# At both gate-and-up starts the third product is moved up behind the fifth, with its operand made straight from PSUM

## The chip, the cores and the metric

The kernel runs on one core of one Trainium2 chip. TensorE (PE in the profile) multiplies into PSUM; VectorE (DVE) and ScalarE (ACT) do elementwise work; SyncE (SP) issues most of the transfers. The metric is device time in microseconds (us) for one execution; lower is better. Before the change the median of three runs is 2316.03 us (2315.48 to 2316.67).

## The reference

One decoder layer is computed in float32, for 1024 positions of width 1024: a gated feed-forward block (width 2816), a mixer, a second feed-forward block, a final normalisation. The change touches only the start of the two feed-forward blocks:

```python
def swiglu(h, w_gate, w_up, w_down):
    a = jnp.einsum("bld,df->blf", h, w_gate)
    b = jnp.einsum("bld,df->blf", h, w_up)
    return jnp.einsum("blf,fd->bld", jax.nn.silu(a) * b, w_down)
...
    x = x + 0.5 * swiglu(rms_norm(x, ffn1_norm[i]), ffn1_w_gate[i], ffn1_w_up[i], ffn1_w_down[i])
...
    x = x + 0.5 * swiglu(rms_norm(x, ffn2_norm[i]), ffn2_w_gate[i], ffn2_w_up[i], ffn2_w_down[i])
```

## The kernel before, in words

**Seven products in place of eight.** Every gate or up multiplication is cut into 2 x 2 blocks and done by Strassen and Winograd's scheme. The normalised input gives blocks r11 and r21 (first half of the positions, first and second half of the features, made in `b_first`) and r12 and r22 (second half of the positions, in `b_second`), and sums of them are the right operands of products 1 to 7; `b_op(H, m)` holds operand m as a rounded float32r part (`bh`) and the rest (`bl`). The weights give left operands the same way (`ah`, `al`), made by `a_ops`. One product is four steps of three matmuls 128x512 (bh by ah, bl by ah, bh by al), twelve in all, and at a start each product is done twice, for the gate and for the up weights: 24 matmuls.

**Banks and running sums.** A product adds into a PSUM bank. Products 1 and 2 share a bank `x` (`ps_pj`). Product 5 goes to bank `z` (gate in `ps_pj`, up in `ps_oo`), is copied out by ScalarE as `r` (L417), and product 3 is later added into the same bank z; so product 3 may write there only after that copy has read it. Before the change products 7 and 4 add into bank `w` (`ps_mx`) and product 6 has a bank `y` of its own (`ps_sc`); VectorE then forms u = y + t1, w = w + u, r = w + r from PSUM.

**The start of a feed-forward block.** `first_products` does products 1 and 2 from the first half of the positions. `b_second` handles the second half: for each of four k it transposes two 128x512 blocks on TensorE (L228, into the two `ps_sc` banks), forms the operands of products 5 and 7 from the first transpose (L300, L304, L306), stores r22 (L302) from the second, and then makes the operands of products 6, 3 and 4 from r11, r22 and r21. `between(0)` and `between(1)` stand for `a_start` with n = 2 and 3, which make the weight operands of the next products, and the loads of the next weight blocks (`a_load`, L325). `gate_up_all` then holds the first gate and up pair by itself (its first loops), before the loop over the 20 further half-blocks. This start occurs twice: near 37 us for the first block (called ffn1 here) and near 1675 us for the second (ffn2).

**What sets the order.** Every engine runs its own list of instructions in order. The kernel is recorded in program order, and a scheduler of the framework then chooses the order in which the instructions stand on each engine, within the bounds that `tc.issue_after` sets. So the two calls of the same functions need not come out in the same order at ffn1 and at ffn2. Pools limit buffers: two `ps_sc`, two `ps_mx`, three `ps_pj`, one `ps_oo`; two buffers each for `ah` and `al`, so the weights of product 4 wait until the matmuls of an earlier group of weights have ended.

Of the kernel before, what the change touches and what calls it, by code (L numbers as in the profile page):

```python
# [11 lines left out]
F32 = mybir.dt.float32  # L12
# [9 lines left out]
P = 128  # L22
# [22 lines left out]
def kernel(  # L45
# [17 lines left out]
    def psum(tag):  # L63
        return ps.tile([P, 512], F32, name="ps_" + tag, tag=tag, bufs=PS_BUFS[tag])
# [159 lines left out]
    def transposed(xns, k):  # L224

        pt = psum("sc")
        for i in range(4):
            T.transpose(pt[:, i * P:(i + 1) * P], xns[i][:, k * P:(k + 1) * P], ident)  # L228
        return pt
# [60 lines left out]
    def b_second(pool, H_ops, x1, wcol, H, r11, r21, r22, between):  # L290

        def put(m, k, src):
            return split2(b_op(H, m)[0][:, k], b_op(H, m)[1][:, k], src)

        first_products(pool, H, H_ops)
        for k in range(4):
            p12 = transposed(x1, k)
            w = wcol[:, k:k + 1]
            t1 = pool.tile([P, 512], F32, name="bs", tag="q")
            V.scalar_tensor_tensor(out=t1, in0=p12, scalar=w, in1=r11[:, k], op0=ALU.mult, op1=ALU.subtract)  # L300
            put(5, k, t1)
            A.mul(out=r22[:, k], in_=transposed(x1, k + 4), mul=wcol[:, k + 4:k + 5])  # L302
            t3 = pool.tile([P, 512], F32, name="bs", tag="q")
            V.scalar_tensor_tensor(out=t3, in0=p12, scalar=w, in1=r22[:, k], op0=ALU.mult, op1=ALU.subtract)  # L304
            hi, lo = put(7, k, t3)
            V.tensor_tensor(out=r11[:, k], in0=r11[:, k], in1=t3, op=ALU.subtract)  # L306
        with tc.issue_after(hi.ins), tc.issue_after(lo.ins):
            between(0)
            for k in range(4):
                put(6, k, r11[:, k])  # L310
            t4 = []
            for k in range(4):
                hi, lo = put(3, k, r22[:, k])
        with tc.issue_after(lo.ins):
            for k in range(4):
                t4.append(pool.tile([P, 512], F32, name="bs", tag="q"))
                V.tensor_tensor(out=t4[k], in0=r21[:, k], in1=r11[:, k], op=ALU.subtract)
        between(1)
        for k in range(4):
            last = put(4, k, t4[k])  # L320
        return last

    def a_load(w, p):
# [4 lines left out]
    def a_ops(pool, *prods):  # L328

        hi = wp.tile([P, 4, 4, P], F32R, name="ah", tag="whi")  # L330
        lo = wp.tile([P, 4, 4, P], F32R, name="al", tag="wlo")
        near = {}
        for i, (raw, m, ops) in enumerate(prods):
            a11, a12 = raw[:, 0:4, 0:P], raw[:, 4:8, 0:P]
            a21, a22 = raw[:, 0:4, P:2 * P], raw[:, 4:8, P:2 * P]

            def summed(x, y, op):
                t = pool.tile([P, 4, P], F32, name="as", tag="q")
                V.tensor_tensor(out=t, in0=x, in1=y, op=op)
                return t  # L340

            if m == 5:
                v = near[id(ops)] = summed(a21, a22, ALU.add)
            elif m == 6:
                if id(ops) in near:
                    v = summed(near[id(ops)], a11, ALU.subtract)
                else:
                    v = summed(a21, a11, ALU.subtract)
                    V.tensor_tensor(out=v, in0=v, in1=a22, op=ALU.add)
                ops["s2"] = v  # L350
            elif m == 7:
                v = summed(a21, a11, ALU.subtract)
            elif m == 3:
                v = summed(a12, ops["s2"], ALU.subtract)
            else:
                v = {1: a11, 2: a12, 4: a22}[m]
            last = split2(hi[:, i], lo[:, i], v)
            ops[m] = hi[:, i], lo[:, i]
        return last


# [6 lines left out]
    def prod(H, bank, ops, m, first=False):  # L368
        (wh, wl), (bh, bl) = ops[m], H[m]
        for k in range(4):  # L370
            a, z = first and k == 0, k == 3
            T.matmul(bank, lhsT=wh[:, k], rhs=bh[:, k], start=a, stop=False, skip_group_check=True)  # L372
            T.matmul(bank, lhsT=wh[:, k], rhs=bl[:, k], start=False, stop=False, skip_group_check=True)  # L373
            T.matmul(bank, lhsT=wl[:, k], rhs=bh[:, k], start=False, stop=z, skip_group_check=True)  # L374
        return bank

    def first_products(pool, H, ops):

        for st in ops:
            st["x"] = prod(H, psum("pj"), st, 1, True)  # L380
            st["t1"] = pool.tile([P, 512], F32, name="m1f")
            A.copy(out=st["t1"], in_=st["x"])
        for st in ops:
            prod(H, st["x"], st, 2)

    def gate_up_all(pool, H, w_gate, w_up, scr, raws, ops, work, tail):
# [6 lines left out]
        def wtile(gate, name):  # L393
            return work.tile([P, 512], F32, name=name, tag="sg" if gate else "mu", bufs=8 if gate else 3)
# [21 lines left out]
            st["r"] = wtile(gate, "r")  # L416
            A.copy(out=st["r"], in_=st["z"])  # L417
        for st in ops:
            st["w"] = prod(H, psum("mx"), st, 7, True)
        for st in ops:  # L420
            st["y"] = prod(H, psum("sc"), st, 6, True)
        for gate, st in zip((True, False), ops):
            st["u"] = wtile(gate, "u2")
            plus(st["u"], st["y"], st["t1"])
            plus(st["w"], st["w"], st["u"])
            plus(st["r"], st["w"], st["r"])
            prod(H, st["z"], st, 3)
        ready((2, 1), (2, 5), (2, 6), (2, 2))
        for st in ops:
# [1086 lines left out]
```

## Time and profile before

| what | value |
|---|---|
| median of three runs | 2316.03 us |
| the profiled execution, its own time | 2315.88 us |
| its span (first to last instruction) | 2314.2 us |
| mean TensorE clock granted | 0.997 of full speed |

One execution is profiled. Its span is 1.7 us below its own time. The profile's page gives for each engine the busy time, the share of the span and the number of instructions, then the span in 40 slices, the chain of work that ended last, and the costliest groups of instructions. The trace behind it can be asked for every instruction in order of time: start, duration, engine, line, operation, tiles out and in, shapes, and in square brackets how long the engine had been idle and what released it. A count such as x2 means that equal neighbours were merged. Matmul durations overlap; what a stream of them costs is read from the distance of their starts.

### The profile page before, as it was taken

To read this page: it belongs to the slowest core of one execution; us is meant where nothing else is said; L and a number is where in the kernel's file an instruction comes from. 1 tells how busy PE (TensorE), PEld (TensorE's weight loads), DVE (VectorE), ACT (ScalarE), POOL (GpSimd) and SP (SyncE) were. 2 spreads that over 40 slices of the span, in tenths; PEclk is the share of its full clock that TensorE was granted. 3 is DMA by queue.
4 is the path that set the end of the run, shared out by engine and by line. 5 is a ranking of instruction groups with operands and counts; after the bars stand their busy time and mean duration, and the time that the engine had idled before them with its cause. 6 is when DMAs were issued, how large, how long until landed. Compare 5 with 4: busy or idle time off the path is not lost.

```text
span 2314.2 us, 31020 instructions
## 1 busy us (share of the span) xinstructions
PE 2270.9 (98%) x11718; PEld 1858.6 (80%) x11718; DVE 1623.5 (70%) x3181; ACT 1082.6 (47%) x1872; POOL 54.0 (2%) x125
## 2 busy tenths in 40 slices
PE   6999999999999999999999999999999999999998
PEld 4888888888878888878788787788878888888886
DVE  7765666667775675668878788888596666656787
ACT  7333333343367785863545555432453333334344
POOL 0000000000000000000000000000000000000000
PEclk9999999999999999999999999999999999999999
DMA  3332323574653322232333322335222323349446
GB/s 111 105 118 92 114 96 109 186 282 124 207 180 99 92 92 61 69 102 74 83 101 75 81 81 58 119 100 190 91 87 96 109 96 110 100 140 327 138 154 214
DMA packets 231435, 281.40 MB, mean 122 GB/s; under 512 B 57448, under 2 KB 164044, under 8 KB 230260
## 3 DMA queue, kind: packets, MB, share of 16 engines
q1 hardware_dynamic: 231028, 279.31, 37.8%
q8 instruction: 92, 1.51, 0.3%
q14 instruction: 59, 0.48, 0.1%
q0 software_dynamic: 256, 0.10, 0.0%
HBM read 211.59 MB, written 67.77 MB: 121 GB/s over the span
## 4 chain that ended last, share of the span: by engine, by line
PE 85%; DVE 8%; ACT 3%; DMA 2%; issue 1%; SPq 0%; POOL 0%; DVEq 0%; ACTq 0%
PE ps_pj L123 9%; PE ps_pj L121 9%; PE ps_pj L122 9%; PE ps_mx L372 5%; PE ps_mx L374 5%; PE ps_mx L373 5%; PE ps_pj L372 3%; PE ps_pj L373 3%; PE ps_pj L374 3%; PE ps_sc L373 3%; PE ps_sc L374 3%; PE ps_sc L372 3%; PE ps_pj L583 2%; PE ps_pj L584 2%; PE ps_pj L582 2%; DMA wst<-in_ffn_w_down_dram 1%
## 5 line engine op out<-in xcount | busy, mean ns | idle before, releaser
L121 PE MATMUL ps_pj<-hhi,whi 128*128 128x512 f32 x832 | 334.3, 402 | 0.8 <-ACT gsb L855 0.8
L123 PE MATMUL ps_pj<-hhi,wlo 128*128 128x512 f32 x832 | 334.4, 402 | 0.0
L122 PE MATMUL ps_pj<-hlo,whi 128*128 128x512 f32 x832 | 331.9, 399 | 0.0
L372 PE MATMUL ps_mx<-bh,ah 128*128 128x512 f32 x512 | 199.4, 390 | 0.0
L373 PE MATMUL ps_mx<-bl,ah 128*128 128x512 f32 x512 | 199.2, 389 | 0.0
L374 PE MATMUL ps_mx<-bh,al 128*128 128x512 f32 x512 | 199.2, 389 | 0.0
L123 PEld LDWEIGHTS ps_pj<-hhi,wlo 128*128 128x128 f32 x832 | 156.7, 188 | 29.6 <-issue 1.9
L121 PEld LDWEIGHTS ps_pj<-hhi,whi 128*128 128x128 f32 x832 | 156.8, 188 | 29.2 <-ACT gsb L855 1.3
L122 PEld LDWEIGHTS ps_pj<-hlo,whi 128*128 128x128 f32 x832 | 156.7, 188 | 29.2 <-issue 1.2
L251 ACT CAST ah<-as 128x512 fp32r<-128x512 f32 x176 | 104.4, 616 | 114.1 <-PE ps_mx L373 106.4
L251 ACT CAST hid<-hraw 128x1024 fp32r<-128x1024 f32 (+1 forms) x84 | 82.4, 981 | 155.3 <-PE ps_oo L584 49.1
L251 ACT CAST ah<-wst 128x512 fp32r<-128x512 f32 x132 | 77.4, 618 | 150.6 <-PE ps_sc L373 122.8
L372 PE MATMUL ps_pj<-bh,ah 128*128 128x512 f32 x368 | 145.1, 395 | 2.7 <-ACT r L417 1.1
L373 PE MATMUL ps_pj<-bl,ah 128*128 128x512 f32 x368 | 144.5, 393 | 0.0
L374 PE MATMUL ps_pj<-bh,al 128*128 128x512 f32 x368 | 143.9, 391 | 0.0
L373 PE MATMUL ps_sc<-bl,ah 128*128 128x512 f32 x336 | 132.8, 395 | 5.3 <-DVE bl L252 5.3
L372 PE MATMUL ps_sc<-bh,ah 128*128 128x512 f32 x336 | 132.4, 394 | 2.0 <-ACT ah L251 2.0
L374 PE MATMUL ps_sc<-bh,al 128*128 128x512 f32 x336 | 132.2, 393 | 0.0
L252 DVE TENSOR_TENSOR hid<-hraw,hid 128x1024 fp32r<-128x1024 f32 (+1 forms) x84 | 95.0, 1131 | 47.3 <-ACT hid L251 46.8
L252 DVE TENSOR_TENSOR al<-as,ah 128x512 fp32r<-128x512 f32 x176 | 116.9, 684 | 3.5 <-ACT ah L251 1.0
L372 PEld LDWEIGHTS ps_mx<-bh,ah 128*128 128x128 f32 x512 | 96.1, 188 | 20.5 <-ACT u L469 0.5
L374 PEld LDWEIGHTS ps_mx<-bh,al 128*128 128x128 f32 x512 | 96.1, 188 | 19.9
(445 smaller groups left out, 5176.4 us busy)
## 6 DMA issues: line engine op xcount, KB each, us to landing
hraw<-hid_scr SPq DMA_DIRECT2D x70, 512.0 KB, 3.7
hid_scr<-hs SPq DMA_DIRECT2D x110, 256.0 KB, 6.4
wst<-in_ffn_w_down_dram SPq DMA_DIRECT2D x50, 512.0 KB, 4.8
wst<-in_ffn_w_gate_dram SPq DMA_DIRECT2D x22, 1024.0 KB, 6.6
wst<-in_ffn_w_up_dram SPq DMA_DIRECT2D x22, 1024.0 KB, 5.4
wst<-in_w_in_dram SPq DMA_DIRECT2D x36, 512.0 KB, 4.8
keep<-in_ffn_w_down_dram SPq DMA_DIRECT2D x20, 512.0 KB, 6.5
wst<-in_w_in_dram SPq DMA_DIRECT2D x8, 1024.0 KB, 5.8
```

Source lines behind the costliest of these rows:

```text
L121: T.matmul(o, lhsT=wh, rhs=mh, start=first, stop=False)
L122: T.matmul(o, lhsT=wh, rhs=ml, start=False, stop=False)
L123: T.matmul(o, lhsT=wl, rhs=mh, start=False, stop=last)
L251: return (A.copy(out=hi, in_=src), V.tensor_tensor(out=lo, in0=src, in1=hi.bitcast(F32), op=ALU.subtract))
L252: V.tensor_tensor(out=lo, in0=src, in1=hi.bitcast(F32), op=ALU.subtract))
L372: T.matmul(bank, lhsT=wh[:, k], rhs=bh[:, k], start=a, stop=False, skip_group_check=True)
L373: T.matmul(bank, lhsT=wh[:, k], rhs=bl[:, k], start=False, stop=False, skip_group_check=True)
L374: T.matmul(bank, lhsT=wl[:, k], rhs=bh[:, k], start=False, stop=z, skip_group_check=True)
L582: T.matmul(bank, lhsT=hh, rhs=wh, start=first and k == 0, stop=False, skip_group_check=True)
L583: T.matmul(bank, lhsT=hh, rhs=wl, start=False, stop=False, skip_group_check=True)
L584: m = T.matmul(bank, lhsT=hl, rhs=wh, start=False, stop=last and k == n - 1, skip_group_check=True)
```

## The change

The third product is moved. In `b_second` its operand (r22, split in `bh` and `bl` of operand 3) is made directly from the transposed block in PSUM: ScalarE multiplies it once into r22 (L304 of the changed kernel) and once into `bh` (L305), and VectorE makes `bl` (L306). The scheme's sums are ordered anew: VectorE subtracts t1 from r22 (L308), which is operand 6; then r11 minus that is operand 7 (L314); r21 minus operand 6 is operand 4 (L320). The weights of product 3 are prepared with those of product 5 (`A_START`), and those of 7 and 6 in the next group. In `gate_up_all` product 3 follows product 5 in bank z; product 6 opens bank y, now in `ps_mx`; t1 is added to it, ScalarE copies it out as u (L427), and products 7 and 4 add into the same bank. The names of the banks in the first hidden block follow.

```diff
-            p12 = transposed(x1, k)
-            w = wcol[:, k:k + 1]
             t1 = pool.tile([P, 512], F32, name="bs", tag="q")
-            V.scalar_tensor_tensor(out=t1, in0=p12, scalar=w, in1=r11[:, k], op0=ALU.mult, op1=ALU.subtract)
+            V.scalar_tensor_tensor(out=t1, in0=transposed(x1, k), scalar=wcol[:, k:k + 1], in1=r11[:, k],
+                                   op0=ALU.mult, op1=ALU.subtract)
             put(5, k, t1)
-            A.mul(out=r22[:, k], in_=transposed(x1, k + 4), mul=wcol[:, k + 4:k + 5])
-            t3 = pool.tile([P, 512], F32, name="bs", tag="q")
-            V.scalar_tensor_tensor(out=t3, in0=p12, scalar=w, in1=r22[:, k], op0=ALU.mult, op1=ALU.subtract)
-            hi, lo = put(7, k, t3)
-            V.tensor_tensor(out=r11[:, k], in0=r11[:, k], in1=t3, op=ALU.subtract)
-        with tc.issue_after(hi.ins), tc.issue_after(lo.ins):
+            p22, w = transposed(x1, k + 4), wcol[:, k + 4:k + 5]
+            hi, lo = (t[:, k] for t in b_op(H, 3))
+            A.mul(out=r22[:, k], in_=p22, mul=w)
+            A.mul(out=hi, in_=p22, mul=w)
+            low = V.scalar_tensor_tensor(out=lo, in0=p22, scalar=w, in1=hi.bitcast(F32),
+                                         op0=ALU.mult, op1=ALU.subtract)
+            V.tensor_tensor(out=r22[:, k], in0=r22[:, k], in1=t1, op=ALU.subtract)
+        with tc.issue_after(low.ins):
             between(0)
             for k in range(4):
-                put(6, k, r11[:, k])
-            t4 = []
+                hi, lo = put(6, k, r22[:, k])
             for k in range(4):
-                hi, lo = put(3, k, r22[:, k])
-        with tc.issue_after(lo.ins):
+                V.tensor_tensor(out=r11[:, k], in0=r11[:, k], in1=r22[:, k], op=ALU.subtract)
+                hi, lo = put(7, k, r11[:, k])
+        with tc.issue_after(hi.ins), tc.issue_after(lo.ins):
+            between(1)
...
-    A_START = (((0, 1), (1, 1), (0, 2), (1, 2)), ((0, 5), (1, 5), (0, 7), (1, 7)),
-               ((0, 6), (1, 6), (0, 3), (1, 3)), ((0, 4), (1, 4)))
+    A_START = (((0, 1), (1, 1), (0, 2), (1, 2)), ((0, 5), (1, 5), (0, 3), (1, 3)),
+               ((0, 7), (0, 6), (1, 7), (1, 6)), ((0, 4), (1, 4)))
...
         for st in ops:
-            st["w"] = prod(H, psum("mx"), st, 7, True)
+            prod(H, st["z"], st, 3)
+        for gate, st in zip((True, False), ops):
+            st["y"] = prod(H, psum("mx"), st, 6, True)
+            plus(st["y"], st["y"], st["t1"])
+            st["u"] = wtile(gate, "u2")
+            A.copy(out=st["u"], in_=st["y"])
         for st in ops:
-            st["y"] = prod(H, psum("sc"), st, 6, True)
-        for gate, st in zip((True, False), ops):
-            st["u"] = wtile(gate, "u2")
-            plus(st["u"], st["y"], st["t1"])
-            plus(st["w"], st["w"], st["u"])
-            plus(st["r"], st["w"], st["r"])
-            prod(H, st["z"], st, 3)
+            prod(H, st["y"], st, 7)
+            plus(st["r"], st["y"], st["r"])
         ready((2, 1), (2, 5), (2, 6), (2, 2))
         for st in ops:
-            prod(H, st["w"], st, 4)
+            prod(H, st["y"], st, 4)
```

How the scheduler places the moved instructions is seen in the built lists. At ffn1, on ScalarE, from the last k of `b_second` on: before (`bh_558` is operand 3, `bh_586` operand 4; `r<-ps_pj` and `r<-ps_oo` are the copies of product 5 for gate and up):

```order
L251 CAST bh_558<-keepx_278 128x512
L251 CAST ah<-wst 128x512 x2
L417 COPY r<-ps_pj 128x512
L417 COPY r<-ps_oo 128x512
L251 CAST bh_586<-bs 128x512 x4
```

and in the changed kernel (`bh_462` is operand 3, `bh_453` operand 5, `bh_540` operand 6, `bh_551` operand 7):

```order
L305 ACTIVATE bh_462<-ps_sc,cols 128x512
L251 CAST bh_453<-bs 128x512
L251 CAST bh_540<-keepx_278 128x512
L420 COPY r<-ps_pj 128x512
L251 CAST ah<-as 128x512
L420 COPY r<-ps_oo 128x512
L251 CAST ah<-as 128x512 x3
L251 CAST bh_551<-keepx_277 128x512 x4
```

At ffn1 the two copies have moved up to stand right behind the operands of products 5 and 6. At ffn2, on ScalarE, the same place before (`bh_14863` is operand 4):

```order
L251 CAST ah<-wst 128x512 x2
L251 CAST bh_14863<-bs 128x512 x4
L417 COPY r<-ps_pj 128x512
L417 COPY r<-ps_oo 128x512
L397 ACTIVATE s_15045<-ps_pj 128x512
```

and in the changed kernel (`bh_14733` is operand 3, `bh_14811` operand 6, `bh_14822` operand 7, `bh_14853` operand 4):

```order
L305 ACTIVATE bh_14733<-ps_sc,cols 128x512
L251 CAST bh_14811<-keepx 128x512
L251 CAST ah<-as 128x512 x4
L251 CAST bh_14822<-keepx 128x512 x4
L251 CAST bh_14853<-bs 128x512 x4
L420 COPY r<-ps_pj 128x512
L420 COPY r<-ps_oo 128x512
L427 COPY u_14936<-ps_mx 128x512
```

There the copies stand, as before, behind the four casts of operand 4. Those casts read `bs`, which VectorE makes (L320). Its list at ffn2 in the changed kernel, from ten rows behind the last row of operand 3 (`bl_14734`) on; `bl_14812`, `bl_14823` and `bl_14854` are operands 6, 7 and 4:

```order
L252 TENSOR_TENSOR bl_14812<-keepx,bh_14811 128x512 x2
L314 TENSOR_TENSOR keepx<-keepx 128x512 x3
L252 TENSOR_TENSOR bl_14823<-keepx,bh_14822 128x512 x3
L314 TENSOR_TENSOR keepx<-keepx 128x512
L406 TENSOR_TENSOR ps_mx<-ps_mx,m1f 128x512 x2
L252 TENSOR_TENSOR bl_14823<-keepx,bh_14822 128x512
L320 TENSOR_TENSOR bs<-r_14512,keepx 128x512 x4
L252 TENSOR_TENSOR bl_14854<-bs,bh_14853 128x512 x4
```

The ten rows ahead of these, from operand 3 on, are of the same size (four sums of weights for products 7 and 6, four rests of these weights, two rows of operand 6), so the last L320 is the 26th. Before, at the same place, the last L317 was the 22nd row behind the last row of operand 7. On TensorE the order at ffn1 is now products 5, 3, 6, 7, 4; at ffn2 it is 5, 6, 3, 7, 4. Before, both had 5 and 7 mixed, then 6, 3, 4.

More of the change, by code (lines that the diff above doesn't have):

```diff
@@ L293, in put @@
             return split2(b_op(H, m)[0][:, k], b_op(H, m)[1][:, k], src)
+        r4 = []
         first_products(pool, H, H_ops)
         for k in range(4):
-            p12 = transposed(x1, k)
-            w = wcol[:, k:k + 1]
             t1 = pool.tile([P, 512], F32, name="bs", tag="q")
-            V.scalar_tensor_tensor(out=t1, in0=p12, scalar=w, in1=r11[:, k], op0=ALU.mult, op1=ALU.subtract)
+            V.scalar_tensor_tensor(out=t1, in0=transposed(x1, k), scalar=wcol[:, k:k + 1], in1=r11[:, k],
+                                   op0=ALU.mult, op1=ALU.subtract)
@@ L311, in b_second @@
-            t4 = []
+                hi, lo = put(6, k, r22[:, k])
             for k in range(4):
-                hi, lo = put(3, k, r22[:, k])
-        with tc.issue_after(lo.ins):
+                V.tensor_tensor(out=r11[:, k], in0=r11[:, k], in1=r22[:, k], op=ALU.subtract)
+                hi, lo = put(7, k, r11[:, k])
+        with tc.issue_after(hi.ins), tc.issue_after(lo.ins):
+            between(1)
             for k in range(4):
-                t4.append(pool.tile([P, 512], F32, name="bs", tag="q"))
-                V.tensor_tensor(out=t4[k], in0=r21[:, k], in1=r11[:, k], op=ALU.subtract)
@@ L318, in b_second @@
-        between(1)
-        for k in range(4):
-            last = put(4, k, t4[k])
+                t4 = pool.tile([P, 512], F32, name="bs", tag="q")
+                V.tensor_tensor(out=t4, in0=r21[:, k], in1=r22[:, k], op=ALU.subtract)
+                r4.append(t4)
+            for k in range(4):
+                last = put(4, k, r4[k])
         return last
@@ L344, in a_ops @@
             elif m == 6:
[L345 to L349, printed above, removed]
+                v = (summed(near[id(ops)], a11, ALU.subtract) if id(ops) in near else
+                     summed(ops["s3"], a22, ALU.add))
                 ops["s2"] = v
             elif m == 7:
-                v = summed(a21, a11, ALU.subtract)
+                v = ops["s3"] = summed(a21, a11, ALU.subtract)
+            elif m == 3 and "s2" not in ops:
+                v = summed(near[id(ops)], a11, ALU.subtract)
+                V.tensor_tensor(out=v, in0=a12, in1=v, op=ALU.subtract)
             elif m == 3:
@@ L442, in gate_up_all @@
         s21 = wtile(True, "s21")
-        silu(s21, g["w"])
+        silu(s21, g["y"])
         plus(g["u"], g["u"], g["z"])
@@ L449, in first_hid @@
             times(s11, u["x"])
-            times(s21, u["w"])
+            times(s21, u["y"])
             plus(u["u"], u["u"], u["z"])
```

## The prediction

> **What bounds the kernel now.** The page comes first: the span, the busy times, the chain of work that ended last.
>
> ```profile
> span 2314.2 us, 31020 instructions
> PE 2270.9 (98%) x11718; PEld 1858.6 (80%) x11718; DVE 1623.5 (70%) x3181; ACT 1082.6 (47%) x1872; POOL 54.0 (2%) x125
> PE 85%; DVE 8%; ACT 3%; DMA 2%; issue 1%; SPq 0%; POOL 0%; DVEq 0%; ACTq 0%
> ```
>
> TensorE is the bound nearly everywhere, so a change matters where TensorE stands idle or runs slowly. The stretches table shows this at the two starts. Its columns are the stretch, its length, busy time and count of PE, PEld, DVE, ACT and POOL, TensorE's granted clock, and the DMA share and rate.
>
> ```profile
> 52.30:57.20 4.90, 1.20 (x4) 0.42 (x3) 4.90 (x9) 4.90 (x11) 0.00 (x0) 0.84 0.00 0
> 57.20:62.50 5.30, 5.30 (x13) 4.19 (x14) 5.30 (x10) 1.43 (x3) 0.00 (x0) 0.50 0.00 0
> 1689.90:1694.60 4.70, 1.11 (x3) 0.37 (x2) 4.70 (x9) 4.67 (x9) 0.00 (x0) 0.94 0.00 0
> 1694.60:1697.40 2.80, 2.78 (x7) 2.20 (x8) 2.80 (x5) 0.00 (x0) 0.00 (x0) 0.50 0.00 0
> 1697.40:1702.40 5.00, 3.87 (x18) 2.85 (x16) 5.00 (x10) 2.99 (x6) 0.00 (x0) 0.99 0.00 0
> ```
>
> In both, TensorE does little for nearly 5 us while DVE is busy throughout; then it goes on at half the clock (1.2 of 2.4 GHz) for 5.3 and 2.8 us. The marks in order of time give the price. At ffn1:
>
> ```profile
> 37.43 0.75 DVE L300 SCALAR_TENSOR_TENSOR bs<-ps_sc,cols,keepx 128x512 f32<-128x512 f32 x1 [1.30 <-PE ps_sc L228]
> 37.65 0.69 ACT L302 ACTIVATE keepx<-ps_sc,cols 128x512 f32<-128x512 f32 x1 [0.75 <-PE ps_sc L228]
> 38.23 0.61 ACT L251 CAST bh<-bs 128x512 fp32r<-128x512 f32 x1
> 38.89 0.50 PE L372 MATMUL ps_pj<-bh,ah 128*128 128x512 f32 x1
> 39.47 0.60 PE L228 MATMUL ps_sc<-ident,xt 128*128 128x128 f32 x4
> 40.10 0.69 ACT L302 ACTIVATE keepx<-ps_sc,cols 128x512 f32<-128x512 f32 x1 [0.33 <-PE ps_sc L228]
> 52.07 0.39 PE L374 MATMUL ps_mx<-bh,al 128*128 128x512 f32 x1
> 64.74 0.39 PE L372 MATMUL ps_pj<-bh,ah 128*128 128x512 f32 x1
> 70.87 0.50 PE L372 MATMUL ps_pj<-bh,ah 128*128 128x512 f32 x1 [0.53 <-ACT ah L251]
> 79.17 0.39 PE L372 MATMUL ps_mx<-bh,ah 128*128 128x512 f32 x1
> ```
>
> Product 5 begins at 38.89 and product 7 ends with the matmul of 52.07. Product 6 should need 24 matmuls and has 12.4 us, until product 3 begins at 64.74. After 79.17 (product 6 of the next half-block) the loop runs. At ffn2:
>
> ```profile
> 1674.70 0.75 DVE L300 SCALAR_TENSOR_TENSOR bs<-ps_sc,cols,keepx 128x512 f32<-128x512 f32 x1 [5.75 <-PE ps_sc L228]
> 1687.37 0.39 PE L374 MATMUL ps_oo<-bh,al 128*128 128x512 f32 x1
> 1687.87 1.28 DVE L339 TENSOR_TENSOR as<-wst 128x512 f32<-128x512 f32 x2
> 1698.70 2.48 DVE L317 TENSOR_TENSOR bs<-r,keepx 128x512 f32<-128x512 f32 x4
> 1699.41 2.42 ACT L251 CAST bh<-bs 128x512 fp32r<-128x512 f32 x4 [4.85 <-DVE bs L317]
> 1701.74 0.58 ACT L417 COPY r<-ps_pj 128x512 f32<-128x512 f32 x1
> 1702.38 0.50 PE L372 MATMUL ps_pj<-bh,ah 128*128 128x512 f32 x1 [1.13 <-ACT r L417]
> 1707.99 0.39 PE L372 MATMUL ps_mx<-bh,ah 128*128 128x512 f32 x1
> 1713.43 0.39 PE L372 MATMUL ps_pj<-bh,ah 128*128 128x512 f32 x1
> 1716.15 0.39 PE L372 MATMUL ps_mx<-bh,ah 128*128 128x512 f32 x1
> ```
>
> Here the last wait is another one. Product 3 (1702.38) waits for the copy of product 5's bank (L417), although product 5 had ended at 1687.37: the copy stands on ACT behind the four casts of operand 4, and these wait for DVE's L317. The 24 matmuls of product 4 go from 1707.99 to 1713.43, 5.44 us or 0.227 each; product 1 of the next half takes 12 more, to 1716.15.
>
> **The change part by part: prices.** DVE and ACT rows of 128x512:
>
> ```profile
> L251 ACT CAST bh<-keepx x16: 611/615/617, 49.7 to 1692.9; 128x512 fp32r<-128x512 f32 x16
> L252 DVE TENSOR_TENSOR bl<-keepx,bh x16: 675/679/681, 56.4 to 1698.1; 128x512 fp32r<-128x512 f32 x16
> L300 DVE SCALAR_TENSOR_TENSOR bs<-ps_sc,cols,keepx x8: 737/742/751, 37.4 to 1683.4; 128x512 f32<-128x512 f32 x8
> L302 ACT ACTIVATE keepx<-ps_sc,cols x8: 687/689/692, 37.6 to 1684.8; 128x512 f32<-128x512 f32 x8
> 1693.89 4.89 DVE L252 TENSOR_TENSOR bl<-keepx,bh 128x512 fp32r<-128x512 f32 x8
> ```
>
> A DVE row in a stream costs 0.60 (8 in 4.89, the last ending later than its successor would start; 18 between 1687.87 and 1698.70 give 0.602), one that reads PSUM about 0.06 more. No matmul is added or removed. DVE has 16 instructions instead of 20 while the transposes last and four more behind them; the weights' sums move by two from the second group to the first, which at ffn2 lies where TensorE is the bound, and at ffn1 fits into this idle time: nothing.
>
> ```profile
> 25.95 0.75 DVE L282 SCALAR_TENSOR_TENSOR bl<-ps_sc,cols,bh 128x512 fp32r<-128x512 f32 x1 [2.02 <-ACT bh L281]
> ```
>
> ACT changes four casts for four activations (0.07 longer each) and has two copies more. One half-block's start has no new transfer.
>
> **ffn1.** The wait for L417 is short here, since the copies now stand right behind product 5's operands. But the phase of products 5 and 3 slows. Per k, TensorE's list has the two first matmuls of product 5, then the transpose for L304 of the next k; ACT has L304, L305, the cast. So the loop is: activation to activation 0.58 (37.65 to 38.23), again 0.58, cast to matmul 0.66 (38.23 to 38.89), matmuls to transpose 0.58 (38.89 to 39.47), transpose to activation 0.63 (39.47 to 40.10): 3.03 us a k, for 6 matmuls and 8 transposes. Product 5 starts 0.58 later (39.47), its last k at 39.47 + 9.09 = 48.56. From there DVE is a chain: its first row behind the last `bl` of product 5 starts 0.8 later (49.4), and the copy u of the up half (L427) stands behind 27 rows: 26 x 0.602 + 0.4 of small waits on ACT + 0.68 gives 66.1; then two casts ahead of it on ACT (1.1) and itself (0.64): product 7 of the up half starts at 67.8. Behind it TensorE has 12 + 24 + 12 matmuls: 48 x 0.227 + 0.1 = 11.0, so the mark of 79.17 falls at 78.8: **-0.4**. The hole and the slow clock of before (7 us) are gone and come back as 3 us in the phase of product 5, 1 at its end, and 1.5 twice ahead of product 7's halves. Bounds: -1.5 (TensorE overlaps what I chained) to +1.0 (0.1 more in each of ten hand-overs).
>
> **ffn2.** The built lists differ: TensorE has 5, 6, 3, 7, 4, and ACT keeps the copies (L420) behind the casts of operand 4, so product 3 waits for DVE's L320, the 26th row of a run without gaps that began with the 19th to 22nd as L317 before. Four rows more are +2.4. The run starts earlier: 16 instructions from 1674.70 on are 8 x 0.66 + 8 x 0.60 = 10.1 of work, and 12.1 with the waits on ACT's rows, when each list is followed row by row with these durations; before, 20 took 13.17. So it starts at 1686.8 (bounds 1684.8 and 1687.9). Then 25 x 0.602 + 0.68 = 1702.5 for the last L320, 0.03 + 0.52 for the last cast, 0.64 for the copy: product 3 at 1703.7, **+1.3**. The same working on the lists of before gives 1702.5, measured 1702.38.
>
> What stands behind that wait has grown: before products 3 and 4 and 12 matmuls, now 3, 7, 4 and those 12. Product 7 was done ahead of the wait and is now behind it: 24 x 0.227 = **+5.4**. And TensorE is idle from the end of product 6 (its last operand is the 12th row of the run, 1694.1, and some eleven matmuls follow: 1696.6) for 7 us, the longest hole of either start. After both holes of before it ran at half clock with a matmul each 0.427:
>
> ```profile
> 1695.21 0.63 PE L374 MATMUL ps_sc<-bh,al 128*128 128x512 f32 x1
> 1695.64 0.63 PE L372 MATMUL ps_sc<-bh,ah 128*128 128x512 f32 x1
> ```
>
> About 6 such matmuls at ffn2, 12 at ffn1, 0.20 each: 1.2 or 2.4. Before at ffn2 this was hidden by the wait for the copy; now 84 matmuls in a row stand behind it. I take the middle, **+1.8** (bounds 0 and 2.4; nothing runs above full clock).
>
> The Trainium skill (TensorE: Matmul & The Clock Gate, Part 1: The HAM clock gate) calls half rate the engine's resting state, left by activity and taken up again in idleness; by that rule the 1.8 stays in the sum, without it the sum of ffn2 is 6.7. The rows of 1694.60 on agree.
>
> A cover to name: the next weights.
>
> ```profile
> 1701.82 0.38 SPq L325 DMA_DIRECT2D wst<-in_ffn_w_gate_dram  x1
> wst<-in_ffn_w_gate_dram SPq DMA_DIRECT2D x22, 1024.0 KB, 6.6
> ```
>
> This load leaves when the weights of product 4 are split, and their buffers come free only when product 3 ends (1703.7 + 5.5 + 1.8 = 1711.0): issue near 1712.4, landed at 1719.0, rounded by 1719.7. Its first matmul is due at 1703.7 + 72 x 0.227 + 1.8 = 1721.9, so 2 us cover it; if the load took 3 us more, 1 us would show.
>
> **Sum.** 2315.88 - 0.4 + 1.3 + 5.4 + 1.8 = 2323.98; the median of the runs shown lies 0.15 above the profiled execution's own time (which is its span of 2314.2 and 1.7 around it): **2324.1 us**, 0.35% slower.
>
> **Rivals.**
> *The copy comes early at ffn2 too* (not slower). If ACT served the copy when product 5 ends, as the lists of ffn1 have it, ffn2 would go like ffn1: from the first DVE row (37.43) to the mark (78.8) 41.4 us, so 1716.1 instead of 1716.15. Sum: 2315.6. It decides when product 3 can start by 1716.15 - 84 x 0.227 = 1697.1; for it speaks that products 5 and 3 need nothing of operand 4; against it, L417 at 1701.74, held 14 us by ACT's list. The Trainium skill (same page, Architectural detail) says ScalarE's queue is strict first in, first out; the row agrees.
> *The clock falls earlier too.* At ffn2 TensorE is thinly used while it waits for the weights of product 6 (near 1685 to 1692, some ten matmuls). At half clock its last 20 matmuls end 4 us later, at 1700.6; L406 of its up half, the 21st row of the run, is due at 1698.8, so 1.8 is added, and the recovery may be the long one (+0.6): 2326.5; with the weights 1 late, 2327.5. For it: 0.94 within the hole at 1689.90; against: two stretches used half, which kept full clock:
>
> ```profile
> 24.80:27.50 2.70, 1.40 (x9) 0.95 (x8) 1.52 (x4) 2.70 (x6) 0.00 (x0) 1.00 0.00 0
> 27.50:30.20 2.70, 1.27 (x9) 0.82 (x9) 2.70 (x6) 2.70 (x7) 0.00 (x0) 1.00 0.00 0
> ```
>
> *The hole costs only itself.* Full clock, run started at 1684.8: 2324.1 - 1.8 - 2.0 = 2320.3.
>
> **How the numbers follow.** Forecast 0.63, clock earlier 0.17, cheap hole 0.07, early copy 0.10, and 0.03 for both holes simply closing (7 us each, faster). The range leaves out the early copy, the closing and part of the cheap hole: 2320.5 to 2328.2. A measurement of this kernel tells about 0.2% (4.6 us) from no change; so slower 0.86, same 0.11, faster 0.03.
>
> **What would show it.** ffn1: no slow clock, product 5 in steps of 3.0 us, idle of about 1.5 before each half of product 7, mark near 78.8. ffn2: the copies behind the casts of operand 4, idle of 7 before product 3 near 1703.5, half clock behind it, and the mark of 1716.15 at about 1724. Wrong: product 3 of ffn2 before 1699, a run of DVE with gaps, or a mark of ffn1 over 81.

## The result, and the profile after

The changed kernel takes **2325.2 us** (median of 6 runs, 2323.58 to 2326.6) against 2315.76 (6 runs, 2314.4 to 2316.67) for the kernel before on the same chip: a ratio of 1.004, 95% interval 1.0027 to 1.0053. It is slower by 0.4%; 2324.1 was predicted. The profiled execution took 2326.6 us, with a span of 2324.9, 10.7 longer than the one of before. The page's lines for the span, the busy times and the chain that ended last:

```profile
span 2324.9 us, 31022 instructions
PE 2274.9 (98%) x11718; PEld 1859.3 (80%) x11718; DVE 1623.7 (70%) x3177; ACT 1083.8 (47%) x1876; POOL 53.8 (2%) x125
PE 85%; DVE 7%; ACT 4%; DMA 2%; issue 1%; SPq 0%; POOL 0%; DVEq 0%; ACTq 0%
```

The shares of the whole program hardly move: TensorE has the same 11718 matmuls and 4 us more of busy time. What the change does is seen at the two starts. In order of time, at ffn1:

```profile
36.52 0.75 DVE L299 SCALAR_TENSOR_TENSOR bs<-ps_sc,cols,keepx 128x512 f32<-128x512 f32 x1 [1.30 <-PE ps_sc L228]
49.95 0.50 PE L375 MATMUL ps_pj<-bh,ah 128*128 128x512 f32 x1 [0.21 <-ACT r L420]
62.41 0.50 PE L375 MATMUL ps_mx<-bh,ah 128*128 128x512 f32 x1 [1.27 <-ACT u L427]
66.86 0.50 PE L375 MATMUL ps_mx<-bh,ah 128*128 128x512 f32 x1 [1.40 <-ACT u L427]
77.90 0.39 PE L375 MATMUL ps_mx<-bh,ah 128*128 128x512 f32 x1
```

Product 3 (49.95) waits 0.21 us for its copy, the two halves of product 7 (62.41, 66.86) wait 1.3 and 1.4 us for the copies u, and the mark (product 6 of the next half-block) comes at 77.90: 41.38 us behind the first DVE row instead of 41.74. Product 5 goes in steps of 3.03 us (38.56, 41.58, 44.61, 47.64), and the granted clock is 1.00 from 36 to 80 us. At ffn2:

```profile
1676.78 0.75 DVE L299 SCALAR_TENSOR_TENSOR bs<-ps_sc,cols,keepx 128x512 f32<-128x512 f32 x1 [5.75 <-PE ps_sc L228]
1700.44 1.53 DVE L406 TENSOR_TENSOR ps_mx<-ps_mx,m1f 128x512 f32<-128x512 f32 x2
1703.24 2.37 ACT L251 CAST bh<-bs 128x512 fp32r<-128x512 f32 x4 [2.06 <-DVE bs L320]
1705.52 0.58 ACT L420 COPY r<-ps_pj 128x512 f32<-128x512 f32 x1
1706.15 0.79 PE L375 MATMUL ps_pj<-bh,ah 128*128 128x512 f32 x1 [4.92 <-ACT r L420]
1713.21 0.39 PE L375 MATMUL ps_mx<-bh,ah 128*128 128x512 f32 x1
1726.81 0.39 PE L375 MATMUL ps_mx<-bh,ah 128*128 128x512 f32 x1
```

The casts of operand 4 wait for DVE's L320, the copy of product 5's bank stands behind them (1705.52), and product 3 starts at 1706.15 after 4.92 us of idle. Product 7 (1713.21) and product 4 follow it, and the mark of 1716.15 is now at 1726.81: 50.03 us behind the first DVE row instead of 41.45. The stretches table (stretch, length, busy time and count of PE, PEld, DVE, ACT, POOL, granted clock, DMA) shows the clock there:

```profile
1687.00:1692.00 5.00, 2.33 (x8) 1.27 (x8) 4.87 (x8) 2.94 (x6) 0.00 (x0) 1.00 0.00 0
1692.00:1697.00 5.00, 4.54 (x11) 2.94 (x10) 5.00 (x10) 1.29 (x3) 0.00 (x0) 0.53 0.00 0
1707.00:1710.00 3.00, 3.00 (x9) 2.33 (x9) 1.25 (x2) 1.06 (x3) 0.00 (x0) 0.60 0.00 0
```

TensorE runs at half clock in most of product 6 (0.53 from 1692 on) and once more in product 3, behind the wait: its first matmuls follow each other at 0.43 us instead of 0.227.

The 10.7 us of span are: -0.91 ahead of ffn1, -0.36 at ffn1, **+3.35 between the mark of ffn1 and the first DVE row of ffn2**, +8.58 at ffn2, +0.04 behind. The 3.35 lie in code that the change doesn't touch and were not predicted, and the profiled execution was the longest of the six. Two places stand out; the first is where the down phase of the first block ends, here with two stretches of after and then the same two of before:

```profile
648.00:652.00 4.00, 1.96 (x10) 1.47 (x9) 3.72 (x12) 2.31 (x3) 0.00 (x0) 0.91 0.86 292
652.00:655.00 3.00, 3.00 (x12) 2.42 (x11) 2.64 (x4) 1.27 (x4) 0.10 (x1) 0.56 0.09 33
```

```profile
648.00:652.00 4.00, 2.77 (x16) 2.04 (x14) 3.72 (x12) 2.69 (x3) 0.00 (x0) 1.00 0.89 312
652.00:655.00 3.00, 2.97 (x17) 2.15 (x14) 3.00 (x4) 2.38 (x4) 0.10 (x1) 1.00 0.21 78
```

After, TensorE did 22 matmuls in these 7 us, 12 of them at a clock of 0.56; before, 33 at full clock. The second is a row of DVE that waits for a transfer, which it did not in the profile of before:

```profile
1604.23 1.41 DVE L1109 SCALAR_TENSOR_TENSOR zg<-ps_mx,cols,zg 128x512 f32<-128x512 f32 x2 [1.06 <-DMA zg<-z_scr]
```

Whether this belongs to the change is the first question for the runs.

### The profile page after: what moved, and what is told of

It reads as the page before. It is cut to its first block, busy times and chain, and to the rows that moved or that the text cites. A ratio compares the mean times of both kernels' runs of the same rounds, so it can differ in the third digit from the quotient of the medians.

```text
span 2324.9 us, 31022 instructions
## 1 busy us (share of the span) xinstructions
PE 2274.9 (98%) x11718; PEld 1859.3 (80%) x11718; DVE 1623.7 (70%) x3177; ACT 1083.8 (47%) x1876; POOL 53.8 (2%) x125
## 4 chain that ended last, share of the span: by engine, by line
PE 85%; DVE 7%; ACT 4%; DMA 2%; issue 1%; SPq 0%; POOL 0%; DVEq 0%; ACTq 0%
PE ps_pj L123 9%; PE ps_pj L121 9%; PE ps_pj L122 9%; PE ps_mx L375 5%; PE ps_mx L377 5%; PE ps_mx L376 5%; PE ps_pj L375 3%; PE ps_pj L376 3%; PE ps_pj L377 3%; PE ps_sc L375 3%; PE ps_sc L377 3%; PE ps_sc L376 3%; PE ps_pj L586 2%; PE ps_pj L587 2%; PE ps_pj L585 2%
## 5 line engine op out<-in xcount | busy, mean ns | idle before, releaser
L375 PE MATMUL ps_mx<-bh,ah 128*128 128x512 f32 x528 | 207.4, 393 | 4.6 <-ACT u L427 2.7
L377 PE MATMUL ps_mx<-bh,al 128*128 128x512 f32 x528 | 206.4, 391 | 0.4 <-DVE al L252 0.4
L376 PE MATMUL ps_mx<-bl,ah 128*128 128x512 f32 x528 | 206.2, 391 | 0.0
L252 DVE TENSOR_TENSOR hid<-hraw,hid 128x1024 fp32r<-128x1024 f32 (+1 forms) x84 | 95.1, 1132 | 49.2 <-ACT hid L251 48.9
L375 PE MATMUL ps_sc<-bh,ah 128*128 128x512 f32 x320 | 124.5, 389 | 0.0
L376 PE MATMUL ps_sc<-bl,ah 128*128 128x512 f32 x320 | 124.5, 389 | 0.0
L377 PE MATMUL ps_sc<-bh,al 128*128 128x512 f32 x320 | 124.5, 389 | 0.0
L252 DVE TENSOR_TENSOR al<-as,ah 128x512 fp32r<-128x512 f32 x176 | 117.7, 686 | 4.4 <-ACT ah L251 2.0
```

What stands on the lines that cost most here:

```text
L252: V.tensor_tensor(out=lo, in0=src, in1=hi.bitcast(F32), op=ALU.subtract))
```

## The experiments

All kernels in one table. Each start is measured in the profile of its run from its first DVE row (L299 in the new order, L300 in the old; the line numbers move where both are kept) to its mark; "middle" is the stretch from the mark of ffn1 to the first DVE row of ffn2; "both starts" is the sum of the two lengths against the 83.19 us of before; the last column is the median of the kernel against that of the kernel before in the same series.

| kernel | ffn1: from, to, us | ffn2: from, to, us | middle, us | both starts | median, against before |
|---|---|---|---|---|---|
| before | 37.43, 79.17, 41.74 | 1674.70, 1716.15, 41.45 | 1595.53 | | |
| changed | 36.52, 77.90, 41.38 | 1676.78, 1726.81, 50.03 | 1598.88 | +8.2 | 2325.20, +9.4 |
| changed, again | 38.18, 79.55, 41.37 | 1673.42, 1723.51, 50.09 | 1593.87 | +8.3 | 2323.77, +7.9 |
| ffn1 only | 37.50, 78.89, 41.39 | 1673.76, 1715.21, 41.45 | 1594.87 | -0.4 | 2315.91, +0.1 |
| ffn2 only | 37.95, 79.49, 41.54 | 1674.74, 1724.80, 50.06 | 1595.25 | +8.4 | 2324.63, +8.8 |
| copies first | 37.82, 79.18, 41.36 | 1674.51, 1718.63, 44.12 | 1595.33 | +2.3 | 2318.47, +2.7 |
| filled hole | 36.96, 78.33, 41.37 | 1672.75, 1721.26, 48.51 | 1594.42 | +6.7 | 2321.55, +6.6 |
| own bank | 37.49, 78.49, 41.00 | 1674.01, 1720.71, 46.70 | 1595.52 | +4.5 | 2321.23, +5.4 |
| late four | 37.62, 78.58, 40.96 | 1673.76, 1717.91, 44.15 | 1595.18 | +1.9 | 2317.02, +2.0 |
| u first | 37.32, 78.34, 41.02 | 1672.13, 1714.52, 42.39 | 1593.79 | +0.2 | 2314.98, 0.0 |
| three split | 37.22, 75.68, 38.46 | 1670.46, 1714.33, 43.87 | 1594.78 | -0.9 | 2314.37, -1.5 |
| before, copies first | 37.91, 79.27, 41.36 | 1674.13, 1715.29, 41.16 | 1594.86 | -0.7 | 2314.92, -0.1 |
| best of each | 38.30, 76.74, 38.44 | 1671.18, 1712.37, 41.19 | 1594.44 | -3.6 | 2312.09, -3.2 |

The medians follow the two starts within 1.3 us in every row. A single median of 11 runs carries about 2 us of uncertainty (the intervals are some 0.09% to each side), one of 4 to 7 runs about 3, so effects under that are read from the lengths in the profiles. Each profile is one execution, and its clock can differ from the next one's, as is seen below.

### The change at one start alone

The functions of the kernel before are kept beside the new ones, and a flag in `ops` chooses: old at ffn2 ("ffn1 only", shown) or old at ffn1 ("ffn2 only").

```diff
-    ops = [{}, {}]
+    ops = [{"old": True}, {"old": True}]
...
-    b_second(npool, ops, x1, nrm[2], H, r11, r21, r22, start_rest(npool, H, ffn2_w_gate[0], ffn2_w_up[0], raws, ops))
+    b_second_old(npool, ops, x1, nrm[2], H, r11, r21, r22, start_rest(npool, H, ffn2_w_gate[0], ffn2_w_up[0], raws, ops))
```

> The new order at ffn1 alone, the old one at ffn2. Theory A (all of the loss is made at ffn2, where the copy of product 5 stands behind the casts of operand 4 on ACT): ffn1 takes 41.4 us from its first DVE row to the mark, ffn2 41.5 as before, so 2315.8 - 0.4 = 2315.4 us, within 1 us. Rival B (part of the loss comes from the 3.4 us by which the unchanged stretch between the two starts was longer in the profiled execution, brought about by the new order at ffn1): that stretch is again near 1599 us instead of 1595.5, and the time is 2318 to 2319.

Measured: 2315.91 us (11 runs), ratio 1.0 (0.9992 to 1.0009); the starts took 41.39 and 41.45 us.

> The old order at ffn1, the new one at ffn2 alone. Theory A: ffn1 41.7 us, ffn2 50.0, so 2315.8 + 8.6 = 2324.4 us, within 1 us. Rival B (the middle stretch grows because of ffn1): the middle is near 1595.5 us in every profile with the old ffn1. Rival C (the loss needs both edits): below 2320.

Measured: 2324.63 us (5 runs), ratio 1.0041 (1.0027 to 1.0054); 41.54 and 50.06. All of the loss is made at ffn2, by the new order there alone. The middle stretch took 1594.87 and 1595.25 us, as in the profile of before: rivals B and C fall.

### The changed kernel once more

> The changed kernel once more, unaltered, for another profile. If the 3.4 us by which the unchanged stretch between the two starts was longer belonged to that one execution: 1595 to 1597 us in this one, ffn1 41.4 and ffn2 50.0 as in the first, time 2324 to 2325. If they belong to the changed kernel: near 1599 again.

Measured: 1593.87 us in the middle, 41.37 and 50.09 at the starts, median 2323.77 (4 runs), ratio 1.0036 (1.0022 to 1.005). The 3.35 us belonged to that one execution: the middle lies between 1593.8 and 1595.5 in the twelve other profiles of the table. What made that one differ stays open.

### Copies first

The casts and low parts of operand 4 are recorded behind the copies of product 5, and queued behind them on ScalarE.

```diff
-            for k in range(4):
-                last = put(4, k, r4[k])
-        return last
+        H["late"] = lambda: [put(4, k, r4[k]) for k in range(4)]
...
-            A.copy(out=st["r"], in_=st["z"])
+            c = A.copy(out=st["r"], in_=st["z"])
+        with tc.issue_after(c.ins):
+            H.pop("late")()
```

> The changed kernel, with the casts of operand 4 queued on ACT behind the two copies of product 5; DVE's list stays as it is. Theory A: at ffn2 the copy now follows the last cast of operand 7, which ended 24.4 us behind the first DVE row, so product 3 starts near 25.1 instead of 29.4, the hole before it shrinks from 4.9 us to about 1, and the 84 matmuls behind it run at full clock: 25.1 + 84 x 0.227 = 44.1 us to the mark instead of 50.0, and 2325.2 - 5.9 = 2319.3 us, within 1.5. Rival D (the run of DVE rows bounds the start, whatever ACT's order is): the interval stays at 49 to 50 and the time at 2324 to 2325.

Measured: 2318.47 us (11 runs), ratio 1.001 (1.0001 to 1.0019); ffn2 44.12 us. In order of time:

```profile
1698.28 0.62 ACT L251 CAST bh<-keepx 128x512 fp32r<-128x512 f32 x1 [1.79 <-DVE keepx L314]
1698.81 0.58 ACT L418 COPY r<-ps_pj 128x512 f32<-128x512 f32 x1
1699.44 0.49 PE L373 MATMUL ps_pj<-bh,ah 128*128 128x512 f32 x1 [0.83 <-ACT r L418]
```

The copy now follows the last cast of operand 7, and product 3 starts 24.93 us behind the first DVE row instead of 29.37, after 0.83 us of idle. From there to the mark it takes 44.12 - 24.93 = 19.19 us, 84 matmuls at 0.228. DVE's rows are the same up to the last L320, so rival D falls: it is the place of the copy in ScalarE's list.

### Filled hole

Twenty matmuls that nothing reads are put behind product 6, at ffn2 alone (`fill` is 20 there, 0 at ffn1; `six(st)` is product 6 of one half, and `last_mm` holds the last matmul that `prod` recorded).

```diff
...
+        if fill:
+            ys = [six(st) for st in ops]
+            spare = psum("sc")
+            with tc.issue_after(last_mm.pop().ins):
+                for k in range(fill):
+                    f = T.matmul(spare, lhsT=ops[0][5][0][:, 0], rhs=H[5][0][:, 0], start=k == 0, stop=k == fill - 1,
+                                 skip_group_check=True)
+        with tc.issue_after(f.ins) if fill else nullcontext():
+            for st in ops:
+                prod(H, st["z"], st, 3)
...
```

> The changed kernel, with 20 matmuls that nothing reads behind product 6 at ffn2, in the idle time before product 3 (0.227 us each at full clock, 4.5 us in all, done before the copy that product 3 waits for). Theory A (of the 8.6 us lost at ffn2, 1.6 to 1.8 are half clock brought on by TensorE's idle time): product 3 starts at 29.1 to 29.4 us behind the first DVE row as in the changed kernel, but runs at full clock: 29.3 + 84 x 0.227 = 48.4 us to the mark instead of 50.0, time 2325.2 - 1.6 = 2323.6. Rival H (the first matmuls behind the wait are slow for another reason): 50.0, time 2325.

Measured: 2321.55 us (7 runs), ratio 1.0026 (1.0015 to 1.0037); ffn2 48.51 us. The rows, and the stretch behind the wait:

```profile
1696.98 4.70 PE L431 MATMUL ps_sc<-bh,ah 128*128 128x512 f32 x20
1702.07 0.50 PE L377 MATMUL ps_pj<-bh,ah 128*128 128x512 f32 x1 [0.39 <-ACT r L422]
```

```profile
1702.00:1707.00 5.00, 4.93 (x22) 4.06 (x23) 2.86 (x5) 2.61 (x6) 0.00 (x0) 1.00 0.00 0
```

Product 3 waits for the same copy until the same point (29.32 us behind the first DVE row), but goes on at full clock, and the mark comes 1.5 us earlier. The same stretch in "ffn2 only", where product 3 starts at 1703.88 after 6.13 us of idle, has a clock of 0.63 and 15 matmuls in place of 22:

```profile
1704.00:1709.00 5.00, 5.00 (x15) 3.98 (x16) 2.30 (x5) 1.78 (x4) 0.00 (x0) 0.63 0.00 0
```

### Own bank

Product 3 gets banks of its own and so waits for no copy. Two additions bring it back in.

```diff
-            prod(H, st["z"], st, 3)
+            st["z3"] = prod(H, psum("sc"), st, 3, True)
...
         plus(g["u"], g["u"], g["z"])
+        plus(g["u"], g["u"], g["z3"])
...
             plus(u["u"], u["u"], u["z"])
+            plus(u["u"], u["u"], u["z3"])
```

> The changed kernel, with product 3 summed in two banks of its own instead of on top of product 5, so that it waits for no copy; two additions on DVE more, far behind. Theory A: at ffn2 product 3 fills the idle time before product 6 and starts within 19 us of the first DVE row. Then product 7 is the next to wait, for the copies u that still stand on ACT behind the casts of operand 4: near 30 us behind the first row, with 60 matmuls behind it, 30 + 13.6 + 0 to 1.6 of half clock = 43.6 to 45.2 to the mark; time 2325.2 - 5.6 = 2319.6, within 1.5. The same at ffn1 as in the changed kernel. Rival D (DVE's rows bound the start): 49 to 50, time 2324 to 2325. Rival E (only the wait for the copy mattered): interval 41.5, time 2316.5.

Measured: 2321.23 us (11 runs), ratio 1.0024 (1.0015 to 1.0033); ffn2 46.70 us.

```profile
1683.81 0.50 PE L375 MATMUL ps_sc<-bh,ah 128*128 128x512 f32 x1 [0.30 <-DVE bs L299]
1701.45 2.37 ACT L251 CAST bh<-bs 128x512 fp32r<-128x512 f32 x4 [2.00 <-DVE bs L320]
1704.68 1.08 ACT L427 COPY u<-ps_mx 128x512 f32<-128x512 f32 x2
1705.33 0.80 PE L375 MATMUL ps_mx<-bh,ah 128*128 128x512 f32 x1 [8.83 <-ACT u L427]
```

Product 3 is done early (from 1683.81 on, mixed with product 5), and TensorE meets the same queue again one product later: product 7 waits 8.83 us for the copies u, which stand behind the same casts. It starts at 31.32 where 30 was expected; 60 matmuls behind it are 13.6; the other 1.8 us are half clock. Rivals D and E fall, and the mechanism is the expected one, but the mark misses its range of 43.6 to 45.2 by 1.5 us: the wait ends 1.3 us later, since two rows for the weights of product 4 (L252, 1.2 us) stand on DVE ahead of L320 here, and the half clock costs 0.2 more than was allowed.

### Late four, and u first

Here the casts and low parts of operand 4, kept in `H["late"]` as in "copies first", go behind the copies u and the sums y + t1.

```diff
...
-            plus(st["y"], st["y"], st["t1"])
+            v = plus(st["y"], st["y"], st["t1"])
...
-            A.copy(out=st["u"], in_=st["y"])
+            c = A.copy(out=st["u"], in_=st["y"])
+        with tc.issue_after(c.ins), tc.issue_after(v.ins):
+            H.pop("late")()
```

> The changed kernel, with the casts and low parts of operand 4 behind the copies u (ACT) and the sums y + t1 (DVE), at both starts. Theory A at ffn2: the copies r stand where they stand in the run with the copies first, so 44.1 us to the mark again. At ffn1 the idle 1.3 and 1.4 us ahead of the two halves of product 7 came from copies u behind casts of operand 4: without them the mark falls between 38.5 and 39.5 us behind the first DVE row instead of 41.4. Time 2318.5 - 2.4 = 2316.1, within 1.5. Rival F (the idle at ffn1 comes from the number of DVE rows ahead of y + t1, which is the same but for four): ffn1 stays at 41 or above, time 2318.5.

Measured: 2317.02 us (11 runs), ratio 1.0008 (0.9999 to 1.0017); 40.96 and 44.15 us. ffn2 is as expected; ffn1 gains 0.4 us, not 2.4. Its rows:

```profile
63.79 2.49 DVE L320 TENSOR_TENSOR bs<-r,keepx 128x512 f32<-128x512 f32 x4
66.20 0.69 DVE L404 TENSOR_TENSOR ps_mx<-ps_mx,m1f 128x512 f32<-128x512 f32 x1
66.92 0.58 ACT L425 COPY u<-ps_mx 128x512 f32<-128x512 f32 x1 [1.55 <-DVE ps_mx L404]
67.56 0.50 PE L373 MATMUL ps_mx<-bh,ah 128*128 128x512 f32 x1 [0.99 <-ACT u L425]
```

The copy u of the up half waits for its sum, and that sum stands on DVE behind the four L320, which this edit left ahead. The wait of the gate half (1.26 us here) stayed too: its copy u stands behind a cast of operand 7 and two casts of weights, in the changed kernel as here, and never stood behind operand 4. So at ffn1 the expectation had the cause wrong, and for the up half it is DVE's list that binds (rival F); at ffn2 it is ScalarE's. The median alone, 2317.0, would have fitted theory A; the lengths in the profile decide.

The next kernel joins "own bank" and "late four" and records the copies r behind the copies u:

```diff
-            st["r"] = wtile(gate, "r")
-            A.copy(out=st["r"], in_=st["z"])
...
+        with tc.issue_after(c.ins):
+            for gate, st in zip((True, False), ops):
+                st["r"] = wtile(gate, "r")
+                A.copy(out=st["r"], in_=st["z"])
```

> The changed kernel with product 3 in banks of its own, and on ACT the copies u first, then the copies r, then the casts of operand 4. Theory A: at ffn2 product 7 now starts when the copies u can, right behind the last cast of operand 7 and two casts of weights, near 26 us behind the first DVE row instead of 31.3; with 60 matmuls behind it 26 + 13.6 + 0 to 1.7 of half clock (the hole before it is 3 to 4 us) = 39.6 to 41.3. At ffn1 38.5 to 40.5. Time 2315.8 - 83.2 + 40.5 + 39.5 = 2312.6, within 2: below the kernel before. Rival D (the DVE rows ahead of the sums y + t1 bind next): product 7 at 28 or later, 43 or more at ffn2, time 2316 or more.

Measured: 2314.98 us (11 runs), ratio 0.9999 (0.999 to 1.0007); 41.02 and 42.39 us.

```profile
1698.10 0.50 PE L373 MATMUL ps_mx<-bh,ah 128*128 128x512 f32 x1 [3.52 <-ACT u L423]
1706.24 0.47 PE L373 MATMUL ps_mx<-bh,ah 128*128 128x512 f32 x1 [0.79 <-DVE r L404]
```

Product 7 starts 25.97 us behind the first DVE row, as expected, but the mark is 1.1 us past the range: 2.0 us of half clock behind the hole of 3.52, and a wait of 0.79 for DVE's L404 that was not counted. ffn1 missed its range too (41.02 against 38.5 to 40.5): product 7 waits 3.06 us there and goes on at a clock of 0.66 for 5 us. So did the time, 2.4 us above the forecast where 2 were allowed. The loss against before is gone; nothing is gained.

### Three split

The up half of product 3 moves into that hole (`last_mm[0]` is the last matmul of product 6).

```diff
...
-        for st in ops:
-            st["z3"] = prod(H, psum("sc"), st, 3, True)
+        ops[0]["z3"] = prod(H, psum("sc"), ops[0], 3, True)
...
             st["y"] = prod(H, psum("mx"), st, 6, True)
+            if not gate:
+                with tc.issue_after(last_mm[0].ins):
+                    st["z3"] = prod(H, psum("sc"), st, 3, True)
```

> The run with the copies u first, with the up half of product 3 moved behind product 6 on TensorE, into the hole before product 7. Theory A (the hole of 3.5 us brought on 1.7 us of half clock at ffn2, and the hole of 3.1 us something like it at ffn1): the hole shrinks to about 1 us, product 7 starts near 26 us behind the first DVE row of ffn2 as before and runs at full clock: 26 + 60 x 0.227 + 0.8 = 40.4 us to the mark instead of 42.4; ffn1 39.4 to 40 instead of 41.0; time 2315.0 - 3 = 2312, within 1.5. Rival H (the half clock stays, because TensorE is thinly used earlier, before product 6, which moves it into product 6): 42 or more at ffn2, 41 at ffn1, time 2315.

Measured: 2314.37 us (11 runs), ratio 0.9995 (0.9986 to 1.0004); 38.46 and 43.87 us. At ffn1 product 7 starts without a wait and the clock stays up: theory A, with 2.6 us gained, more than was expected. At ffn2 the outcome is rival H's: TensorE, served with weights one by one, fell to half clock inside product 6. The stretches of product 6 at ffn1 and at ffn2, and the row of product 7 at ffn2:

```profile
51.70:58.70 7.00, 6.05 (x24) 4.22 (x25) 7.00 (x12) 2.88 (x5) 0.00 (x0) 1.00 0.00 0
1685.20:1693.90 8.70, 7.67 (x24) 5.43 (x25) 8.70 (x15) 3.10 (x6) 0.00 (x0) 0.80 0.00 0
```

```profile
1698.42 0.50 PE L375 MATMUL ps_mx<-bh,ah 128*128 128x512 f32 x1 [1.49 <-ACT u L427]
1706.05 0.47 PE L375 MATMUL ps_mx<-bh,ah 128*128 128x512 f32 x1 [1.86 <-DVE r L406]
```

The same work took 7.0 us there and 8.7 here, product 7 came 2 us later (27.96), and product 4 waited 1.86 us for DVE. The thin use lies inside product 6, though, not ahead of it as rival H had it: from 1680.27 to 1684.7 TensorE ran product 5 and the gate half of product 3 without a gap. Why the clock held at ffn1, with the same waits in product 6, is not shown; the time (2314.4) is past theory A's range.

### Before, copies first

The same edit as in "copies first", on the kernel before.

> The kernel before, with the casts of operand 4 queued on ACT behind the two copies of product 5, the same edit as in the run with the copies first. Theory A: the 1.13 us that product 3 of ffn2 waited for its copy go, product 3 follows product 6 near 26.4 us behind the first DVE row, and 26.4 + 60 x 0.227 = 40.1 to 40.4 instead of 41.45; ffn1 as before. Time 2314.6, which the runs can hardly tell from 2315.8; the interval in the profile decides. Rival G (the place in ACT's queue did not bind the kernel before): 41.4 to 41.5.

Measured: 2314.92 us (11 runs), ratio 0.9998 (0.9989 to 1.0007); ffn2 41.16 us. The stretch of product 6, and the start of product 3:

```profile
1694.00:1699.50 5.50, 5.44 (x13) 4.33 (x14) 5.50 (x11) 0.48 (x2) 0.00 (x0) 0.51 0.00 0
```

```profile
1701.69 0.39 PE L370 MATMUL ps_pj<-bh,ah 128*128 128x512 f32 x1
```

The wait for the copy is gone: product 3 follows product 6 with no idle time. But product 6 itself ended 1.2 us later than in the profile of before, at half clock for longer, so 0.3 us remained of the 1.1 expected, between theory A and rival G. In "ffn1 only", whose ffn2 is that of before, product 6 also ended late, and the wait for the copy covered it. So the copy's place bound the kernel before in the execution first profiled, but product 6 comes right behind it as a bound, and its end moves with TensorE's clock.

### Best of each

"Three split" at ffn1, "before, copies first" at ffn2, chosen by the flag of the first experiment.

> At ffn1 the arrangement of the run with product 3 split around product 6 (38.5 us there), at ffn2 that of the kernel before with its copies ahead of the casts of operand 4 (41.2). Theory A (what a start costs is decided by its own lists, so the two add up): 38.5 and 41.2 against 41.7 and 41.5 before, time 2315.9 - 3.5 = 2312.4, within 1.2. Rival I (what one start gains is lost behind it): 2315 to 2316.

Measured: **2312.09 us** (11 runs, 2310.94 to 2314.42) against 2315.27, ratio 0.9987 (0.9978 to 0.9996); 38.44 and 41.19 us. It is ahead of both kernels, of the changed one by 13 us (whose median comes from another series).

## Why the prediction was right

The time lay 1.1 us above the forecast, within the range, and ffn2 took 8.58 us more where 8.5 were predicted. Step by step:

- **Product 3's start, +1.3.** It came 29.37 us behind the first DVE row instead of 27.68: +1.7, and in the second profile of the changed kernel 29.15: +1.5. The reason was the predicted one; "copies first" moved product 3 forward by 4.4 us by changing the order of the copies and the casts of operand 4 alone. The Trainium skill (TensorE: Matmul & The Clock Gate, Architectural detail) calls ScalarE's queue strictly first in, first out, and this run agrees. The first profile's extra 0.2 come from the two L406, which took 1.53 us in place of 1.30 in the second, because product 6 ended late.
- **Product 7 behind the wait, +5.4.** In "own bank" product 3 is taken out from behind the wait in turn: 24 x 0.227 = 5.4 us less behind it, and 2 us of later start, leave 3.3 less (50.03 to 46.70; the clock costs about the same in both).
- **Half clock behind the hole, +1.8.** "Filled hole" removed it and left product 3's start where it was: 1.5 us. From the rows, 50.03 - 29.37 - 84 x 0.227 = 1.6 in the first profile, and 50.09 - 29.15 - 84 x 0.227 = 1.9 in the second. By the Trainium skill's rule that half rate is the engine's resting state (same page, Part 1: The HAM clock gate) a hole filled with matmuls keeps the rate up; the clock of 1.00 behind the filled hole, against 0.63, agrees.
- **ffn1, -0.4.** 41.38 against 41.74, with product 7 of the up half 30.34 us behind the first DVE row (66.86) where 67.8 - 37.43 = 30.4 was worked out. But the old order at ffn1 took 41.54 and 41.36 in two other profiles, so the gain is nearer to 0.2, below what a median can show: "ffn1 only" is at +0.1. The way there came out as worked out: steps of 3.03 us in product 5, no slow clock, and idle times of 1.27 and 1.40 where 1.5 was said twice.
- **The next weights** stayed hidden. The cast of the first ones in the changed kernel:

```profile
1720.10 1.15 ACT L251 CAST ah<-wst 128x512 fp32r<-128x512 f32 x2 [2.61 <-DMA wst<-in_ffn_w_gate_dram]
```

They landed by 1720.1, and product 1, which reads them, ran on at 1724.1 without a wait.

One step was off without showing in the sum, and that was luck. **The rival that the clock falls earlier** came true: product 6 lost the full clock in the changed kernel's first profile (0.53 from 1692 on) and, for a shorter stretch, in its second, whose rows these are:

```profile
1688.25 0.50 PE L375 MATMUL ps_mx<-bh,ah 128*128 128x512 f32 x1 [1.93 <-ACT ah L251]
1692.10 0.63 PE L377 MATMUL ps_mx<-bh,al 128*128 128x512 f32 x1
1696.06 0.39 PE L377 MATMUL ps_mx<-bh,al 128*128 128x512 f32 x1
```

Product 6 ended 24.5 and 23.0 us behind the first DVE row, where the forecast had 21.9 and the rival 25.9. That is why the idle time before product 3, said to be 7 us, was 4.92 and 6.13. The second L406 waits for that end and was due near 24.3 (1697.7 in the second profile), so only the first profile shows a cost, 0.2 us. The forecast put this fall at nothing and the rival at up to 3.4 us; by the same chain of rows, a fall 1 us longer would have come nearly whole into the time.

The rival of an early copy is what "copies first" made true in part: 44.1, not 41.4, since its copies still stood behind the casts of operand 7.

The 1.1 us between forecast and median are within the uncertainty: the two medians of the changed kernel are 2325.2 and 2323.8.

## What to carry to other kernels

When code is moved into a new order, look at where each small copy stands in its engine's list at every call of the function, and at what the instructions ahead of it wait for: one copy of 0.58 us behind four casts held 84 matmuls here, and the same code was harmless at the other call. Removing one such wait tends to uncover the next in the same list (r, then u, then DVE's sums), so compare the start of the product that waits with the end of the product ahead of it before an edit is priced. And before a difference in untouched code, like the 3.35 us here, is put down to a change, take a second profile.

## What the runs showed of the hardware

The same matmuls in the same order do not get the same clock in every execution: product 6 of the changed kernel at ffn2, with the same waits ahead of it, took 9.25 us from its first matmul to its last in one profile (1691.59 to 1700.84) and 7.81 in the other (1688.25 to 1696.06). And the clock can fall without TensorE ever being idle for long: in "three split" product 6 had a granted clock of 1.00 at ffn1 and 0.80 at ffn2, with waits of 0.4 to 0.6 us between its matmuls in both. In the middle of the program the profile of the changed kernel has a clock of 0.56 at 652 us behind an idle time of 2.04 us, and that of before 1.00 behind 1.23. What a fall costs when work stands behind it was steadier at ffn2: 1.5 to 2.0 us in the changed kernel, "ffn2 only", "own bank" and "u first".
